# Gate projections by seven block products in a stage of their own ahead of attention, with the fill of the attention heads dealt anew

## The chip, the cores and the metric

The kernel runs on one core of one Trainium2 chip. The metric is the time of one execution on the device in microseconds, the median of the runs shown. Engines are named as in the profile: PE (TensorE, its weight loads apart as PEld), DVE (VectorE), ACT (ScalarE), POOL (GpSimd) and SP, whose queue issues the DMAs.

## The reference, cut to what matters

One decoder layer, sequence 1024, width 1024, in float32: half a SwiGLU feed-forward, two attention mixers side by side with gates, half a SwiGLU feed-forward, and a gated per-layer input.

```
x = x + 0.5 * swiglu(rms_norm(x, ffn1_norm), ffn1_w_gate, ffn1_w_up, ffn1_w_down)
h = rms_norm(x, mix_norm)
fq, fk, fv, f_logit, sq, sk, sv, g_fox, g_sb = split_columns(h @ w_in)
y_fox = forgetting_attention(rms_norm(fq), rms_norm(fk), fv, log_sigmoid(f_logit + forget_bias))
y_sb  = stick_breaking_attention(sq, sk, sv)
merged = sigmoid(g_fox) * (y_fox @ w_branch_fox) + sigmoid(g_sb) * (y_sb @ w_branch_sb)
x = x + merged @ w_out
x = x + 0.5 * swiglu(rms_norm(x, ffn2_norm), ffn2_w_gate, ffn2_w_up, ffn2_w_down)
out = x + sigmoid(rms_norm(x, ple_norm) @ w_ple_gate) * (p @ w_ple_proj)
```

Each mixer has 8 heads of 64. The gates `g_fox` and `g_sb` are 2 x 1024 of the 5128 columns of `w_in`. Forgetting attention is causal softmax with a bias from cumulated forget logs; stick-breaking attention weighs key s for query t by `beta[t,s] * prod_{s<j<t} (1 - beta[t,j])`, a running product from the diagonal to the left.

## The kernel before, in words

**Precision.** Every float32 operand is split into a high part in fp32r and a low remainder; a product is three: high x high, high x low, low x high. `split` (L103) does that: ACT copies the high part, DVE (or POOL, for weights, `wlow`, L139) subtracts it.

**Feed-forwards.** `ffn` computes up and gate as pairs of 128-column tiles for two halves of the tokens. All pairs but the first use seven block products instead of eight (Winograd's scheme): 12 products of 128x512 for each block, 84 for a pair where plain sums take 96. The operand sums on the token side (`combo_a`, `t`, `l`, `u`, `s`, `d`, `e`) are made once, at the stage's start; the sums on the weight side (`sums`, `last_sum`) for each pair. The first pair is done in plain sums (`plain`, L428) while the token sums are built. The products are at L473. `second_entry` opens the second feed-forward in the last products of the output projection; the down projection (`make_down`, L368) has the scheme too.

**The mix stage.** At the end of the first `ffn`, `mix_start` normalises x, transposes it to `hT`, and computes the first v group (`u1`) and the first q/k pair (`u2`). What else `w_in` gives is cut into units for PE, each with its weights' load and split: `v_units` (8 units of 24 products, 256 columns), `fox_qk_units` (the same), `fox_stack_units` (two units of 4 transposes), `sb_stack_units` (two units of 24 products of 128x512, for a stick-breaking head's q and k) and `g_units` (a gate tile of 128 columns: two half-tile units of 24 products of 128x512, L708). A gate unit ends with a copy (L831) or a sigmoid (L833) and a store to the scratch `gates`; `gated` loads fox gates again and applies the sigmoid there.

**Attention.** Sixteen heads in order, 0 to 7 forgetting, 8 to 15 stick-breaking; each has four steps c = 0 to 3, of two query blocks of 128. A step is `scores` for its own rows (L944, L945) and then `apply` for the step before it. In `apply`, for each pair of key blocks from the diagonal down to 0: PE transposes the weights (`transposes`, L996), ACT makes the high part (L998), DVE the low part (L999), PE multiplies with v (`values`, L1018). In stick-breaking heads `scores` has two sigmoids for each segment (ACT, L952 and L953), running products by scans on DVE (L920) and multiplications on POOL (L967, L971). The scans of the even row block come at once; those of the odd one, `right` and `left`, are put into `later` and stand in DVE's order between the low parts of `apply`. At each step's end the head's result is copied out (L1037, L1038).

Each head h has a list `fill[h]` of such units, of what later heads need, and of gates. `take` hands out 1/22 of the list's cost after each row block's scores, after each pair's transposes and before the last values, so the list lasts to the head's end:

```
        turn_and_scan(c)
        for kpair in range(c - 1, -1, -1):
            turn_and_scan(kpair)
            values(kpair + 1)
        for part in later:
            part()
        fill()
        values(0)
```

**What orders the work.** PE's order is the program's, held by `order`; so are the order of scans and low parts of stick-breaking heads on DVE, and of their high parts on ACT. The rest of attention is placed by the framework's scheduler; inside `ffn` and its entry and end the order is written out by hand. SBUF tiles come from tags with a fixed number of buffers (`BUFS`; PT has 3), and a new tile waits until the readers of the old one are done.

Of the kernel before, what the change touches and what calls it, by code (L numbers as in the profile page):

```python
# [18 lines left out]
P = 128  # L19
# [7 lines left out]
NH = 8  # L27
# [4 lines left out]
        "Q": 2, "KH": 2, "KL": 2, "Y": 2, "PT": 3}  # L32
# [4 lines left out]
def tile_hybrid_decoder_layer(  # L37
# [223 lines left out]
    def halves(N):  # L261
        return [(n["hi"], n["lo"]) for n in N]
# [117 lines left out]
    def ffn(N, wg, wu, wd, next_gain, resid, hid, tags, entry, tail):  # L380

        wsrc = [kp(w[0]) for w in (wg, wu)]
        wdown = wd[0].rearrange("(j k p) n -> k p j n", k=2, p=P)
        LA = 4
        nm_ = 2 * NF  # L390
# [4 lines left out]
        seqn += [(n, 1), (n - 1, 4), (n, 2), (n, 6), (n, 5), (n, 7), (n - 1, 3), (n, 3), (n, 4)]  # L395
# [9 lines left out]
        def load(n):  # L405
            f0 = n // 2 * 256
            W[n] = {"r": [slot(t, [P, 4, 256]) for t in tags["raw"].get(n, (("WH", "WH"), ("KH", "KL"))[n % 2])]}
            for kh in range(2):
                nc.sync.dma_start(W[n]["r"][kh][:], wsrc[n % 2][:, 4 * kh:4 * kh + 4, f0:f0 + 256])
# [23 lines left out]
        def silu(f_, half):  # L433
            if 0 not in E:
                E[0] = [slot(t, [P, 2, 512]) for t in ("GF", "RN")]
            nc.scalar.activation(E[0][f_][:, half, :], bank_of.pop("plain")[:], AF.Silu)
# [11 lines left out]
        def prep(n, m):  # L448
# [9 lines left out]
            if m == 3 and n + 2 < nm_:  # L458
                load(n + 2)
# [19 lines left out]

        def right(t, b, k):  # L480
            if isinstance(t, list):
                return t[2 * b + k // 2][:, k % 2, :]
            return t[:, b, k, :]

        def evict(n, m, ps):
# [8 lines left out]
            elif m == 7:  # L494
                nc.scalar.copy(e2[:, 1, :], ps[:])
                nc.vector.tensor_add(e2[:, 1, :], e2[:, 1, :], bank_of[n, "d"][:])
# [27 lines left out]
        C = {"w": {}, "t1": {}}  # L524

        def combo_a(q):

            h = N[1]["h"][q]
            cs = slice(q * P, (q + 1) * P)
            if q == 0:  # L530
                B[1], B[2] = N[0]["B"]
                B[3] = [slot("T", [P, 2, 512], F32R) for _ in range(4)]
                B["12"] = slot("X", [P, 2, 4, 512], F32R)
            w = C["w"][q] = slot(tags["w"][q], [P, 2, 4, P])
            v12, v22 = (turn(h, b, bank(cyc("t", ("pf", "av", "pf", "sc", "pt", "av", "pt", "sc")))) for b in range(2))
            nc.scalar.copy(w[:, 0], v12)
            nc.scalar.copy(w[:, 1], v22)
            split(B["12"][:, 0, :, cs], B["12"][:, 1, :, cs], w[:, 0], nc.scalar, nc.vector)
            for i in range(2):
                split(B[3][i][:, :, cs], B[3][2 + i][:, :, cs], w[:, 1, 2 * i:2 * i + 2], nc.scalar, nc.vector)  # L540

        def combo_t(q):

            cs = slice(q * P, (q + 1) * P)
            if q == 0:
                B[5] = slot("H", [P, 2, 4, 512], F32R)
            if q % 2 == 0:
                C["t1"][q // 2] = slot(("RN", "GF")[q // 2], [P, 2, 4, P])
            w, t1 = C["w"][q], C["t1"][q // 2][:, q % 2]
            nc.vector.tensor_sub(t1, w[:, 0], f(B[1][:, 0, :, cs]))  # L550
            nc.vector.tensor_sub(t1, t1, f(B[1][:, 1, :, cs]))
            nc.scalar.copy(B[5][:, 0, :, cs], t1)

        def combo_l(q):

            cs = slice(q * P, (q + 1) * P)
            nc.vector.tensor_sub(B[5][:, 1, :, cs], C["t1"][q // 2][:, q % 2], f(B[5][:, 0, :, cs]))

        def combo_u(q):

            w, t1 = C["w"][q], C["t1"][q // 2][:, q % 2]
            nc.vector.tensor_sub(w[:, 0], w[:, 1], w[:, 0])
            nc.vector.tensor_sub(w[:, 1], w[:, 1], t1)

        def combo_s(q, m):

            cs = slice(q * P, (q + 1) * P)
            if q == 0:
                B[m] = slot("H" if m == 6 else "X", [P, 2, 4, 512], F32R)
            split(B[m][:, 0, :, cs], B[m][:, 1, :, cs], C["w"][q][:, 7 - m], nc.scalar, nc.vector)  # L570

        def combo_d(q):

            cs = slice(q * P, (q + 1) * P)
            w = C["w"][q]
            nc.vector.tensor_sub(w[:, 0], f(B[2][:, 0, :, cs]), w[:, 1])
            nc.vector.tensor_add(w[:, 0], w[:, 0], f(B[2][:, 1, :, cs]))

        def combo_e(q):
            cs = slice(q * P, (q + 1) * P)  # L580
            if q == 0:
                B[4] = slot("X", [P, 2, 4, 512], F32R)
            split(B[4][:, 0, :, cs], B[4][:, 1, :, cs], C["w"][q][:, 0], nc.scalar, nc.vector)

        down = make_down(wdown, hid, [(0, 4), (4, 7), (7, 11)], 0.5, ("Y", "PT"))
        nxt = []

        def last_norms(i, t):
            if i == 4:
                norm_stat(nxt[0], t, ("PT", "PT", "KH", "KL")[t])  # L590
            elif i == 5:
                norm_mul(nxt[0], t)
            elif i == 6:
                if t == 3:
                    norm_post(nxt[0], 2, ps1)
                norm_stat(nxt[1], t, ("GF", "RN", "KH", "KL")[t])
                if t:
                    if t < 3:
                        norm_mul(nxt[1], t - 1)
                    norm_post(nxt[0], (None, 0, 1, 3)[t], ps1)  # L600
                for call in tail.get((i, t), ()):
                    call(nxt)

        manual[0] = True
        with tc.manual_schedule():
            entry(dict(a=combo_a, t=combo_t, l=combo_l, u=combo_u, s=combo_s, load=load, prep=prep, sums=sums, last_sum=last_sum, plain=plain, silu=silu, product=product, evict=evict))
            for s, (n, m) in enumerate(seqn):
                evict(n, m, product(n, m))
                if s == 0:
                    sums(2, nc.vector)  # L610
                    for q in range(4):
                        combo_s(q, 7)
                elif s == 2:
                    last_sum(1, nc.vector)
                    last_sum(2, nc.vector)
                if 1 < s < 6:
                    combo_d(s - 2)
                if 2 < s < 7:
                    combo_e(s - 3)
                if s + LA < len(seqn):  # L620
                    prep(*seqn[s + LA])
# [22 lines left out]
            for s, (c, i) in enumerate(steps):  # L644
# [18 lines left out]
                if final:  # L663
                    if i == 3:
                        nxt.append(norm_begin(X[0], next_gain))
                        nxt.append(norm_begin(X[1], next_gain, nxt[0]))
                    for call in tail.get(i, ()):
                        call(X)
                for t in range(4):
                    matmuls(t)  # L670
                    evict_down(t)
                    if final:
                        last_norms(i, t)
            norm_mul(nxt[1], 2)
            norm_mul(nxt[1], 3)
            tail["end"](X, nxt)
        manual[0] = False
        return X, nxt
# [302 lines left out]
    def apply(step, fill, later=()):  # L981
# [48 lines left out]
        for part in later:  # L1030
            part()
# [517 lines left out]
```

## Time and profile before

| | before |
|---|---|
| median of 3 runs | 2273.08 us (2272.70 to 2273.09) |
| profiled execution | 2274.11 us, its span 2272.4 us |
| granted TensorE clock | 1.0 |
| heads 0 to 7 (forgetting) | 755.7 to 1049.7 us |
| heads 8 to 14 (stick-breaking) | 1049.7 to 1341.7 us |
| head 15 to the end of attention | 1341.7 to 1393.3 us |

The span runs from the first instruction of the profiled execution to the last; the execution's time is somewhat longer. In rows of the timeline the first number is the start in us, the second the length; in brackets stands how long the engine had been idle and what ended that. In rows of groups the numbers after the bar are busy us in all and mean ns of one, and then idle time before them. In rows of windows stand the stretch, its length, and the busy time of PE, PEld, DVE, ACT and POOL, then the clock, the DMA engines' share and GB/s.

### The profile page before, as it was taken

The numbers are of one execution on the slowest core, as the hardware profiler recorded it, in microseconds if no ns is written. First come the engines' busy times: TensorE is split into PE (matmuls) and PEld (weight loads), VectorE is DVE, ScalarE is ACT, GpSimd is POOL, SyncE is SP. The second block draws the span as 40 slices with busy tenths as digits, with TensorE's granted clock in tenths as the row PEclk, the third lists the DMA queues.
The fourth block names the chain that finished last, engine by engine and source line by source line (L and its number), as shares of the span: only waits on it lengthen the run. The fifth ranks groups of instructions, "written<-read, shape, count | busy, mean of one in ns | idle before, by whom it ended". The sixth has DMA issues, their size and how long they took to land. (4 is left out here: it accounts for less than half of the span.)

```text
span 2272.4 us, 30639 instructions
## 1 busy us (share of the span) xinstructions
PE 2248.2 (99%) x11462; PEld 1911.9 (84%) x11462; DVE 1462.3 (64%) x2199; ACT 977.4 (43%) x1741; POOL 828.8 (36%) x762
## 2 busy tenths in 40 slices
PE   8999999999999999999999999999999999999999
PEld 6888888888899999988988888888888888888888
DVE  8845555688863466666667676889655555778753
ACT  6333333333353555555555564246333333434431
POOL 2344444300033456554645644410544444200121
PEclk9999999999999999999999999999999999999999
DMA  4232323484333322132224245822423232756132
GB/s 139 99 120 85 124 84 125 152 302 171 103 122 121 103 80 75 48 89 70 52 56 116 61 144 176 299 109 65 139 84 125 84 125 80 263 194 218 60 103 84
DMA packets 187655, 275.49 MB, mean 121 GB/s; under 512 B 27113, under 2 KB 109417, under 8 KB 187506
## 3 DMA queue, kind: packets, MB, share of 16 engines
q1 hardware_dynamic: 187504, 273.53, 35.9%
q8 instruction: 90, 1.47, 0.3%
q14 instruction: 59, 0.48, 0.1%
q10 hardware_dynamic: 2, 0.00, 0.0%
HBM read 189.83 MB, written 75.27 MB: 117 GB/s over the span
## 5 line engine op out<-in xcount | busy, mean ns | idle before, releaser
L368 PE MATMUL ps<-H,H 128*128 128x512 f32 x2184 | 497.7, 389 | 1.2 <-DVE X L376 1.2
L368 PEld LDWEIGHTS ps<-H,H 128*128 128x128 f32 x2184 | 409.4, 188 | 86.7 <-issue 2.0
L473 PE MATMUL ps<-H,WL 128*128 128x512 f32 x1008 | 239.3, 389 | 0.8 <-ACT WL L105 0.8
L473 PEld LDWEIGHTS ps<-H,WL 128*128 128x128 f32 x1008 | 189.1, 188 | 40.4 <-ACT WL L105 1.2
L708 PE MATMUL ps<-H,WH 128*128 128x512 f32 x768 | 210.3, 401 | 1.1 <-DVE PT L831 1.1
L708 PEld LDWEIGHTS ps<-H,WH 128*128 128x128 f32 x768 | 136.4, 188 | 24.1 <-DVE PT L831 1.5
L139 POOL TENSOR_TENSOR WL<-RAW,WH 128x512 fp32r<-128x512 f32 (+1 forms) x108 | 127.4, 1200 | 77.5 <-ACT WH L129 71.9
L139 POOL TENSOR_TENSOR WL<-Y,WH 128x512 fp32r<-128x512 f32 (+1 forms) x10 | 14.4, 1466 | 382.6 <-ACT WH L129 382.6
L999 DVE TENSOR_TENSOR PT<-ps,PT 128x512 fp32r<-128x512 f32 (+1 forms) x160 | 101.1, 633 | 76.1 <-ACT PT L998 75.1
L473 PE MATMUL ps<-H,Q 128*128 128x512 f32 x600 | 143.1, 389 | 0.0
L376 DVE SCALAR_TENSOR_TENSOR X<-ps,X 128x512 f32<-128x512 f32 x168 | 109.0, 685 | 50.9 <-PE ps L368 50.9
L700 PE MATMUL ps<-WH,H 128*128 128x256 f32 (+1 forms) x896 | 132.0, 287 | 1.9 <-DVE X L106 1.0
L473 PEld LDWEIGHTS ps<-H,Q 128*128 128x128 f32 x600 | 112.6, 188 | 23.4
L998 ACT CAST PT<-ps 128x512 fp32r<-128x512 f32 (+1 forms) x160 | 87.3, 548 | 95.8 <-PE ps L996 92.3
L473 PE MATMUL ps<-X,WL 128*128 128x512 f32 x504 | 121.1, 389 | 0.0
L700 PEld LDWEIGHTS ps<-WH,H 128*128 128x128 f32 x896 | 116.9, 190 | 3.7 <-DVE X L106 1.4
L1018 PE MATMUL ps<-PT,X 128*128 128x256 f32 (+1 forms) x640 | 106.2, 283 | 6.1 <-DVE PT L999 6.0
L473 PEld LDWEIGHTS ps<-X,WL 128*128 128x128 f32 x504 | 94.6, 188 | 19.6
L1018 PEld LDWEIGHTS ps<-PT,X 128*128 128x128 f32 x640 | 94.5, 190 | 19.1 <-DVE PT L999 9.7
L708 PE MATMUL ps<-H,WL 128*128 128x512 f32 x384 | 108.3, 398 | 0.0
L957 POOL TENSOR_TENSOR T<-T,l 128x128 f32<-128x128 f32 (+3 forms) x64 | 73.3, 1150 | 88.5 <-DVE l L956 86.1
L269 POOL TENSOR_TENSOR PT<-GF,RN 128x512 f32<-128x512 f32 x20 | 33.1, 1655 | 186.0 <-DVE GF L516 101.8
(400 smaller groups left out, 4735.3 us busy)
## 6 DMA issues: line engine op xcount, KB each, us to landing
hidden<-PT SPq DMA_DIRECT2D x40, 512.0 KB, 3.1
WH<-in_ffn_w_gate_dram SPq DMA_DIRECT2D x38, 512.0 KB, 5.3
Q<-hidden SPq DMA_DIRECT2D x24, 512.0 KB, 6.1
hidden<-RN SPq DMA_DIRECT2D x22, 512.0 KB, 2.7
RAW<-in_w_in_dram SPq DMA_DIRECT2D x22, 512.0 KB, 4.3
KH<-in_ffn_w_up_dram SPq DMA_DIRECT2D x20, 512.0 KB, 6.2
KL<-in_ffn_w_up_dram SPq DMA_DIRECT2D x20, 512.0 KB, 6.8
T<-in_ffn_w_down_dram SPq DMA_DIRECT2D x20, 512.0 KB, 4.3
```

What stands on the lines that cost most here:

```text
L139: ins = eng_lo.tensor_sub(lo[part], raw[part], f(hi[part]))
L269: eng.tensor_add(s12[:, 0, :], g1[:, 1, :], g2[:, 1, :])
L368: pe(nc.tensor.matmul(groups[g][t][:], act[:, a, k, t * P:(t + 1) * P], wt[:, b, k, :], start=(fresh and n == 0), stop=(i in (6, 1, 4) and ...
L376: nc.vector.scalar_tensor_tensor(xs, groups[g][t][:], scale, xs, ALU.mult, ALU.add)
L473: pe(nc.tensor.matmul(ps[:], hl[:, a, k, :], rhs(m, b, k), start=(first and i == 0), stop=(final and i == 11), skip_group_check=True))
L700: pe(nc.tensor.matmul(ps[:, :n], hT[t // 4][a][:, k, (t % 4) * P:(t % 4 + 1) * P], w[k // 4][b][:, k % 4, :n], start=(i == 0), stop=(i == ...
L708: pe(nc.tensor.matmul(ps[:], w[a][:, k, :], hT[half][b][:, k, :], start=(i == 0), stop=(i == 23)))
L957: nc.gpsimd.tensor_mul(T[:, :n], T[:, :n], l[:].broadcast_to([P, n]))
L998: high = nc.scalar.copy(pt[:, 0, :width], ps[:, :width])
L999: low = nc.vector.tensor_sub(pt[:, 1, :width], ps[:, :width], f(pt[:, 0, :width]))
L1018: pe(nc.tensor.matmul(o, lh, r, start=(kpair == c and i == 0), stop=(kpair == 0 and i == 3)))
```

## The change

- The gate tiles 0 to 11 leave attention. After the first `ffn` comes a stage of six pairs of gate tiles (`NG = 6`), written like the start of the second feed-forward, from which the shared parts are taken out (`make_up`, `up_order`, `up_begin`, `up_step`, `up_first`, `products`). Pair 0 is done in plain sums, pairs 1 to 5 by seven block products. Its results get the sigmoid at once and are stored.
- `hT` is now read from the operands of that stage (`B[1]`, `B[2]`, `B["12"]`, `B[3]`), whose homes are other tags than in the feed-forwards. All of `u1` runs at the stage's end, all of `u2` at the start of attention.
- Gate tiles 12 to 15 stay fill units. The fill lists are dealt anew, with stacks further behind their q and k units.
- `values` of a key pair come one more pair behind its transposes, and PT has five buffers.
- The sigmoid of fox gates moves from `gated` to `g_units`.

```diff
-        "Q": 2, "KH": 2, "KL": 2, "Y": 2, "PT": 3}
+        "Q": 2, "KH": 2, "KL": 2, "Y": 2, "PT": 5}
...
             g = slot("PT", [P, 512])
-            if m < KD:
-                nc.vector.tensor_copy(g[:], ps[:])
-            else:
-                order("act", nc.scalar.activation(g[:], ps[:], AF.Sigmoid))
+            order("act", nc.scalar.activation(g[:], ps[:], AF.Sigmoid))
...
             turn_and_scan(kpair)
-            values(kpair + 1)
+            if kpair + 2 <= c:
+                values(kpair + 2)
         for part in later:
             part()
+        if c:
+            values(1)
         fill()
         values(0)
...
+    NG = 6
...
+        tags_g = {"raw": UP_TAGS["raw"], "sum": UP_TAGS["sum"], "w": UP_TAGS["w"], "hl": hl, "t1": "X",
+                  "B": {"12": "H", 3: "H", 5: ("Y", "Y", "PT", "PT"), 6: ("T",) * 4, 7: "X", 4: "X"}}
+        F = make_up(N, lambda n: kp(win)[:, :, GFOX + n * 256:GFOX + n * 256 + 256], NG, tags_g, AF.Sigmoid, gate_out, load_qk)
...
+        def end():
+            up_first(N, F)
+            seqn = up_order(NG)
+            L = len(seqn)
+            for s, (n, m) in enumerate(seqn):
+                evict(n, m, F.product(n, m))
+                F.begin(s)
+                if s + 4 < L:
+                    F.prep(*seqn[s + 4])
+                if s == L - 16:
+                    raws["v"] = [wraw_load(pieces[kh], 4, 256 + NH, "PT") for kh in range(2)]
+                elif s == L - 5:
+                    mx["v"]["w"] = [wsplit(raws["v"][kh], 4, 256 + NH, ("T", "WL")) for kh in range(2)]
+                elif s == L - 2:
+                    mx["qk"]["w"] = [wsplit(raws["qk"][kh], 4, 256, tags[kh]) for kh in range(2)]
...
+            for _, g in mx["u1"]:
+                run(g)
...
-        run_all(g0[:1] + f0[:1] + p0[1:3] + g0[1:] + f0[1:] + p0[3:] + g1[:1] + p1 + g1[1:])
-        fill = []
-        fill.append(mix(fst(1), fox_qk_units(fox_pairs[1], qk[1])))
...
-        u, g6 = sst(8), g_units(6)
-        fill.append(u + g6)
-        u, g7, g8 = sst(9), g_units(7), g_units(8)
-        fill.append(u + g7 + g8[:1])
-        u, uv = sst(10), v_units(SV + 256, 0, vs1)
-        fill.append(u + g8[1:] + uv[:4])
-        u, g9 = sst(11), g_units(9)
-        fill.append(uv[4:] + u + g9[:1])
-        u, g10 = sst(12), g_units(10)
-        fill.append(u + g9[1:] + g10)
-        u, g11, g12 = sst(13), g_units(11), g_units(12)
-        fill.append(u + g11 + g12[:1])
-        u, g13 = sst(14), g_units(13)
-        fill.append(u + g12[1:] + g13)
-        u, g14, g15 = sst(15), g_units(14), g_units(15)
-        fill.append([u[0], g14[0], g15[0], u[1], g14[1]])
-        fill.append(g15[1:] + fox_branch[:7])
+        run_all(f0[:1] + p0[1:7] + f0[1:] + p0[7:] + p1)
...
+        fill = [mix(f[0], qk1[:7]),
+                qk1[7:] + vx[:1] + f[1][:1] + vx[1:4] + f[1][1:],
+                mix(f[2], vx[4:] + uq2[:3]),
+                uq2[3:] + g12[:1] + f[3][:1] + g12[1:] + f[3][1:],
+                mix(f[4], uq3[:6]),
+                uq3[6:] + vy[:1] + f[5][:1] + vy[1:4] + f[5][1:],
+                mix(f[6], vy[4:] + g13[:1]),
+                g13[1:] + s8,
+                s9 + vz[:2],
+                vz[2:5] + s10,
+                vz[5:] + s11,
+                s12 + g14[:1],
+                g14[1:] + s13,
+                s14 + g15[:1],
+                g15[1:] + s15,
+                fox_branch[:7]]
...
         nc.sync.dma_start(dst, gd[gate * KD + m, :, half * 512:half * 512 + 512])
-        order("act", nc.scalar.activation(dst, dst, AF.Sigmoid))
         nc.vector.tensor_mul(dst, dst, ps[:])
...
-    nc = _bacc.Bacc("TRN2", target_bir_lowering=False, num_devices=1, dynamic_dma_scratch_size=8192)
+    nc = _bacc.Bacc("TRN2", target_bir_lowering=False, num_devices=1, dynamic_dma_scratch_size=4096)
```

In the entries of the old list that are left out here stood gate tiles 2 to 5; tiles 0 and 1 were computed ahead of the list.

More of the change, by code (lines that the diff above doesn't have):

```diff
@@ L522, in hidden_sums @@
             del E[n], E[n - 1]
[L524 to L540, printed above, removed]
```

501 lines of the change are left out of this document (287 added, 214 removed).

## The prediction, made before the changed kernel was run

> **What bounds the kernel now.** I read the page first, then the chain of waits in order of time, then windows cut by stage and by step of attention, then the timelines of one step.
>
> ```profile
> span 2272.4 us, 30639 instructions
> ...
> PE 2248.2 (99%) x11462; PEld 1911.9 (84%) x11462; DVE 1462.3 (64%) x2199; ACT 977.4 (43%) x1741; POOL 828.8 (36%) x762
> ...
> PE 46%; DVE 2%; ACT 1%; issue 0%; DVEq 0%; ACTq 0%
> ```
>
> TensorE is busy 99% of the span, and the 46% is only as far back as the chain could be followed; DVE's 2% is the first hint of a second bound. The next views say how fast PE runs undisturbed, and how full the others are in attention.
>
> ```profile
> 1566.89 394.40 PE ps L473 x1740
> 755.72:1049.73 294.01, 289.80 (x2074) 271.34 (x2073) 180.11 (x563) 159.91 (x346) 166.75 (x169) 1.00 0.25 70
> 1049.73:1341.74 292.01, 288.42 (x1639) 249.26 (x1637) 195.59 (x279) 160.13 (x337) 164.70 (x181) 1.00 0.29 80
> 1341.74:1393.33 51.59, 49.22 (x272) 41.89 (x271) 40.20 (x54) 34.96 (x70) 28.25 (x34) 1.00 0.56 185
> PE ps L1018 <- DVE PT L999: 6.0, 10, 1.7
> ```
>
> The first row is from the chain in order of time: 1740 products of 128x512 in 394.40 us, 0.2267 us each. The next three are windows (length, then PE, weight loads, DVE, ACT, POOL busy, granted clock): the eight forgetting heads 0 to 7, the stick-breaking heads 8 to 14, and head 15 to the end of attention. PE is covered by fill, but DVE is at 61%, 67% and 78%. The last row, from the waits of PE in attention, is the only large one: value products (L1018) waiting ten times, 6.0 us in all, for the low part that DVE makes (L999). So PE's number of products bounds the kernel, with little lost; and what attention can do with less fill is set by DVE.
>
> **The change, part by part.**
>
> *Fewer products.* Before, 12 gate tiles cost 12 x 48 = 576 products of 128x512. After, the first two tiles are four plain sums of 24, and five pairs take seven blocks of 12: 96 + 420 = 516. At 0.2267 us the 60 fewer are **-13.6 us**. The stage is 516 x 0.2267 = 117 us of PE ahead of attention, and 130.6 us of fill leaves it.
>
> *The stage itself.* It runs the code that opens the second FFN, whose first 120 us and whose entry the trace shows:
>
> ```profile
> 1535.28 1.09 PE L228 MATMUL ps<-identf,PT 128*128 128x128 f32 x8 [0.99 <-DVE H L106]
> 1536.77 1.09 PE L228 MATMUL ps<-identf,PT 128*128 128x128 f32 x8 [0.40 <-ACT Q L536]
> 1566.90:1687.00 120.10, 120.10 (x531) 99.47 (x531) 81.89 (x104) 47.59 (x85) 47.23 (x33) 1.00 0.30 103
> 603.00:640.00 37.00, 37.00 (x165) 30.64 (x164) 28.65 (x31) 19.10 (x24) 10.84 (x12) 1.00 0.38 129
> RAW<-in_w_in_dram SPq DMA_DIRECT2D x22, 512.0 KB, 4.3
> ```
>
> After the entry PE stood busy for all 120.10 us, with DVE at 68% beside it: the operand sums (113 more DVE instructions and 16 fewer copies in the whole kernel) are hidden there, and would cost their time only if PE had waits. The entry idled 0.99 + 0.40 us; the old end of the first FFN, 603 to 640, idled nothing. So **+1.4 us**, bounds +1 and +5 (the homes of the operands differ, and the v and q/k weights are now split at its end). The loads and stores of x, gates and weights go through SP's queue as before, two tiles, some 14 products or 38 us, ahead, and land in 4.3 us: nothing.
>
> *Less fill in stick-breaking heads: the term that decides.* A head's fill is dealt in 22 equal portions: 7 in step c0, 4 in c1, 5 in c2, 6 in c3. Heads 8, 11, 12, 13 and 14 go from five half-tile units to three: 2 x 24 x 0.2267 = 10.9 us less, each portion 1.24 to 0.74 us. Heads 9 and 10 lose one such unit and one unit of 24 products of 256 columns, counted at half that price: 8.2 us; head 15 loses 5.4 us. Here are head 13's four steps (windows), then rows of its c3 from the timelines of DVE, ACT, PE and POOL, one scan of head 12, and a group of heads 8 to 14:
>
> ```profile
> 1258.55:1271.56 13.01, 13.01 (x76) 11.21 (x75) 5.51 (x10) 5.06 (x12) 3.43 (x6) 1.00 0.31 93
> 1271.56:1278.40 6.84, 6.84 (x36) 5.68 (x35) 3.89 (x8) 4.67 (x9) 4.08 (x5) 1.00 0.00 0
> 1278.40:1287.62 9.22, 9.22 (x52) 7.97 (x51) 8.39 (x11) 5.72 (x13) 7.77 (x9) 1.00 0.43 116
> 1287.62:1299.51 11.89, 11.89 (x65) 10.03 (x64) 9.47 (x11) 7.73 (x15) 8.43 (x8) 1.00 0.13 44
> ...
> 1293.24 0.56 DVE L999 TENSOR_TENSOR PT<-ps,PT 128x384 fp32r<-128x384 f32 x1 [0.74 <-ACT PT L998]
> 1293.72 1.12 DVE L920 TENSOR_TENSOR_SCAN RN<-GF,mask_sb 128x128 f32<-128x128 f32 x1
> 1294.87 1.01 DVE L920 TENSOR_TENSOR_SCAN RN<-GF,RN 128x383 f32<-128x383 f32 x1
> ...
> 1296.38 2.03 DVE L920 TENSOR_TENSOR_SCAN RN<-GF,RN 128x512 f32<-128x512 f32 x1
> 1298.33 0.66 DVE L999 TENSOR_TENSOR PT<-ps,PT 128x512 fp32r<-128x512 f32 x1
> ...
> 1288.27 0.55 ACT L952 ACTIVATE GF<-ps 128x448 f32<-128x448 f32 x1
> ...
> 1292.21 0.63 ACT L833 ACTIVATE PT<-ps 128x512 f32<-128x512 f32 x1
> 1292.68 0.53 ACT L998 CAST PT<-ps 128x384 fp32r<-128x384 f32 x1
> ...
> 1298.85 0.82 PE L1018 MATMUL ps<-PT,X 128*128 128x256 f32 x4
> ...
> 1293.55 1.00 POOL L971 TENSOR_TENSOR T<-T,RN 128x384 f32<-128x384 f32 x1
> 1248.50 0.43 DVE L920 TENSOR_TENSOR_SCAN RN<-GF,mask_sb 128x128 f32<-128x128 f32 x1 [1.10 <-ACT GF L952]
> ...
> L785 DVE TENSOR_TENSOR KL<-ps,KH 64x512 fp32r<-64x512 f32 x14 | 9.7, 695 | 0.3
> ```
>
> With the smaller portions PE's own work is 13.01 - 3.5 = 9.5, 6.84 - 2.0 = 4.9, 9.22 - 2.5 = 6.7 and 11.89 - 3.0 = 8.9 us. DVE has 5.5, 3.9, 8.4 and 9.5 us: in c0 and c1 it has room, in c2 and c3 together it has 17.9 us against 15.6. Every step ends with values(0), which needs the last low part; that low part stands behind all scans of the step in DVE's order, and the change keeps that order. So what DVE lacks in c2 and c3 cannot be paid back in c0.
>
> How much is it? In c3 the chain runs thus: eight sigmoids from 0.65 us after the step's start to 4.6 (ACT with hardly a break, so less fill does not hurry them), the high part 0.5, then DVE without a pause from the first low part (1293.24) to the last (1298.99), 5.75 us, then the last values, 0.45. That is 11.3 us against PE's 8.9: 2.4 us. It falls to 1.0 if the scans run at their shortest: 0.43 us for the 1.12, and for 512 columns at the pace of the 383 in 1.01, 1.35 for the 2.03. PE already started its last values at 1298.85, before that low part was done: there is no slack to spend. In c2, 8.4 against 6.7 bounds the loss by 0 and 1.7; I take 0.6, as part of the last scan runs over into c3. In c1 I take 0.1 (bounds 0 and 0.5). The stacks make it worse at the upper end: one half of the next head's (two subtractions of about 0.7 us) now falls behind c2's last scan in DVE's order as built, where it stood in c0 and c1 (+1.4). So 3.1 us a head, bounds 0.8 and 4.5: five heads 15.5; heads 9 and 10, with three quarters of the cut, 1.5 each (0 and 2.5); head 15, where DVE's 40.20 of 51.59 us is full already, 2.5 (1.7 and 4.5). The longest wait that stands there now, 1.7 us, may go. **+19 us**, bounds +4 and +32.
>
> The value products now come a key pair later (five PT buffers instead of three). That takes away waits for a low part in the middle of a step; the last one has only a portion and four products more ahead of it, which is in the 8.9 us.
>
> On the scans: one of 128 columns took 0.43 us with POOL idle (1248.50), and 1.12 when a POOL multiplication had begun 0.17 us earlier; it ended 0.3 us after that one did. I keep the long ones, since the same multiplications follow the same scans after the change. [...]
>
> *Less fill in forgetting heads.* Their fill goes from about 23 to between 14 and 25 us; head 1 loses most, three units of 24 products of 256 columns, 8.2 us (a window, and a group):
>
> ```profile
> 789.58:827.09 37.51, 37.03 (x303) 36.46 (x302) 23.51 (x72) 21.16 (x46) 22.17 (x23) 1.00 0.21 57
> L883 ACT ACT_TABLE_LOAD x1 | 1.3, 1283 | 0.0
> ```
>
> 37.5 - 8.2 = 29.3 us of PE against 23.5 of DVE: room is left, and there are no scans between low parts. I take 0.5 us in five heads and 1 in head 1, **+3.5 us** (bounds -1, if the later values remove waits, and +6). Four sigmoids of gate tiles 12 and 13 now fall between exponentials of these heads: eight table loads more there, 1.28 us each on ACT (one more, at the gate stage, is hidden). ACT has 16 us free even in that head; I take **+1 us**, bounds 0 and 8 x 1.28 = 10.3.
>
> *Sum.* -13.6 + 1.4 + 19 + 3.5 + 1 = **+11 us** on the profiled execution, 2274.1 (span 2272.4 and 1.7 around it), that is 2285; the median of the three runs is 2273.1, 1 us lower: **2284 us**.
>
> **Rivals.** *PE still decides.* If ACT's and DVE's chains start as much earlier as PE does, and the scans run at their short durations, the losses are the lower bounds: -13.6 + 1.4 + 4 - 1 + 0 = -9, **2264 us**, faster. For it speaks that the later values and five buffers loosen every wait but the last of a step; against it, 17.9 us of DVE in 15.6 of PE. It decides when c2 and c3 together end less than 1 us late in each head.
>
> *The attention heads fall apart.* The stack halves lie in DVE's way in every c2 and the table loads, 10.3 us on ACT, hold up the high parts that values wait for: -13.6 + 3 + 28 + 6 + 8 = +31, **2304 us**. For it: ACT's 23.2 us would fill 77% of head 13; against it: the loads fall in only three heads. [...]
>
> *It comes out even.* Half of the 19 us in the stick-breaking heads, 1.4 at the entry and 2.5 in the forgetting heads make 13.4 against the 13.6: **2273 us**; the fill would then be worth to attention just what the blocks save.
>
> **How the numbers follow.** A measurement here tells about 0.2%, 4.5 us, from no change. Forecast 0.50, PE decides 0.30, even 0.12, falls apart 0.08. Slower than 2277.6: 0.50 + 0.08 = 0.58; within: 0.12; faster: 0.30. The forecast's own range is 2275 to 2298; as 0.30 lies on the other side, the range reaches from 2262 to 2304.
>
> **What would show it.** Right: the new stage runs PE full at 0.2267 us a product for 117 us, with under 3 us of idle time at its entry; heads 11 to 14 last 33 to 34 us instead of 41; PE's waits for the low part grow from 6 to over 20 us, nearly all at the ends of c2 and c3; DVE is at 80 to 88% of these heads. Wrong: these heads last 31 us or less (PE decides); or PE's idle time lies in the gate stage, or in heads 3, 6 and 7 behind a table load.

## The result, and the profile after

| | before | after |
|---|---|---|
| median | 2273.06 us (2272.70 to 2273.09, 4 runs) | 2324.7 us (2322.22 to 2327.65, 4 runs) |
| profiled execution, its span | 2274.11, 2272.4 us | 2324.22, 2322.3 us |

The ratio is 1.0228, 95% interval 1.0215 to 1.024: the kernel became slower by 51.6 us. The sign was forecast, the size was not: 11 us, and the upper end of the range was 2304.

First the page's head and busy lines of the changed kernel, then windows of its gate stage, heads 0 to 7, heads 8 to 14, and head 15 with the rest of attention.

```profile
span 2322.3 us, 30570 instructions
...
PE 2255.0 (97%) x11402; PEld 1909.7 (82%) x11402; DVE 1526.4 (66%) x2296; ACT 1018.1 (44%) x1819; POOL 811.4 (35%) x747
```

```profile
640.00:757.00 117.00, 115.99 (x543) 96.22 (x542) 86.04 (x134) 61.32 (x117) 15.64 (x17) 1.00 0.34 114
851.30:1144.30 293.00, 267.25 (x1927) 249.84 (x1926) 173.00 (x550) 168.57 (x355) 159.08 (x162) 0.98 0.22 60
1144.30:1392.60 248.30, 223.95 (x1330) 192.12 (x1329) 198.14 (x277) 150.14 (x324) 150.27 (x170) 0.99 0.25 69
1392.60:1442.70 50.10, 46.74 (x247) 39.30 (x247) 40.61 (x56) 24.46 (x52) 29.57 (x31) 0.95 0.52 176
```

TensorE has 60 instructions fewer, as planned, and is full in the gate stage. In attention it is not: 25.8 us of heads 0 to 7 and 24.4 of heads 8 to 14 are empty, and the granted clock, 1.00 throughout before, is 0.98, 0.99 and 0.95. Set beside the times of before, with a gate tile at 48 products of 0.2267 us, the difference splits thus:

| stretch | length before | length after | TensorE's work moved | lost |
|---|---|---|---|---|
| start to the first scores | 755.7 | 851.3 | 516 products in, tiles 0 and 1 out: +95.2 | 0.4 |
| heads 0 to 7 | 294.0 | 293.5 | three tiles out: -32.6 | 32.1 |
| heads 8 to 15 | 343.6 | 297.9 | seven tiles out: -76.2 | 30.5 |
| the rest | 879.1 | 879.6 | none | 0.5 |

The moved work is -13.6 in all, the loss 63.5, together the 49.9 us by which the spans differ. So heads 0 to 7 gave nothing back at all for three gate tiles less. The 32.1 us lost there lie in all eight heads, 1.8 to 7.2 us in each, with the most in heads 4 and 6. TensorE stands still 21.5 us longer than before, and its remaining products take 10.6 us longer, in part because of the half clock shown below. (The windows above end 0.4 us before head 8 begins; the table goes by the first scores.)

Line numbers are higher in the changed kernel: L1092, L1094, L1095 and L1114 are transposes, high parts, low parts and values; L799 and L807 the products of fill units; L889, L106 and L929 the evictions of stacks, v and gates; L1016 the scans.

These are the waits of TensorE in heads 0 to 7 of the changed kernel (us in all, times, the longest), then the largest of heads 8 to 15:

```profile
PE ps L799 <- DVE KL L889: 7.1, 3, 2.8
PE ps L1092 <- DVE PT L1095: 5.3, 6, 1.4
PE ps L799 <- DVE X L106: 4.5, 4, 1.8
PE ps L807 <- ACT PT L929: 1.6, 1, 1.6
PE ps L1114 <- DVE PT L1095: 1.6, 2, 1.2
PE ps L1114 <- ACT PT L1094: 1.5, 1, 1.5
PE ps L1092 <- POOL T L1053: 1.2, 2, 0.8
```

```profile
PE ps L1114 <- DVE PT L1095: 23.2, 24, 1.8
```

The second is the wait that the prediction named: value products for the last low part, 6.0 us before, 23.2 now. The first list has no leader: fill units that wait for the eviction of a stack (KL), of v (X) or of a gate (PT, L929), transposes and values that wait for high and low parts. And this is how such a wait looks in the timeline of TensorE, at the start of head 4:

```profile
999.83 0.66 PE L901 MATMUL ps<-identf,RN 128*128 128x128 f32 x4 [0.94 <-ACT PT L929]
1003.26 0.98 PE L799 MATMUL ps<-WH,H 128*128 128x256 f32 x3 [2.78 <-DVE KL L889]
...
1004.46 1.70 PE L799 MATMUL ps<-WH,H 128*128 128x256 f32 x7
...
1010.11 1.08 PE L799 MATMUL ps<-WH,H 128*128 128x256 f32 x7
```

After 0.94 and 2.78 us of standing still, seven products take 1.70 us; the same seven take 1.08 later. The granted clock is 0.5 from 1002.1 to 1008.9 us, and in four other places of attention: 23.9 us in all at half speed.

### The profile page after: what moved, and what is told of

Read it like the earlier page. It is cut to its first block, busy times and chain, and to the rows that moved or that the text cites. A ratio compares the mean times of both kernels' runs of the same rounds, so it can differ in the third digit from the quotient of the medians.

```text
span 2322.3 us, 30570 instructions
## 1 busy us (share of the span) xinstructions
PE 2255.0 (97%) x11402; PEld 1909.7 (82%) x11402; DVE 1526.4 (66%) x2296; ACT 1018.1 (44%) x1819; POOL 811.4 (35%) x747
## 4 chain that ended last, share of the span: by engine, by line
PE 85%; DVE 8%; ACT 4%; issue 2%; POOL 1%; DMA 0%; SPq 0%; ACTq 0%; DVEq 0%; POOLq 0%
PE ps L556 38%; PE ps L454 21%; PE ps L799 7%; PE ps L1556 4%; DVE RN L1016 3%; PE ps L1361 3%; PE ps L1114 2%; PE ps L807 2%; PE ps L506 2%; PE ps L1092 2%; DVE PT L1095 1%; PE ps L959 1%; PE ps L228 1%; PE ps L1040 1%; PE ps L1041 1%
## 5 line engine op out<-in xcount | busy, mean ns | idle before, releaser
L556 PE MATMUL ps<-H,WL 128*128 128x512 f32 x1116 | 265.0, 389 | 0.8 <-ACT WL L105 0.8
L556 PEld LDWEIGHTS ps<-H,WL 128*128 128x128 f32 x1116 | 209.4, 188 | 44.7 <-ACT WL L105 1.2
L1095 DVE TENSOR_TENSOR PT<-ps,PT 128x512 fp32r<-128x512 f32 (+1 forms) x160 | 99.9, 629 | 61.9 <-ACT PT L1094 60.9
L556 PEld LDWEIGHTS ps<-H,Q 128*128 128x128 f32 x612 | 114.9, 188 | 23.9
L799 PE MATMUL ps<-WH,H 128*128 128x256 f32 x768 | 121.7, 296 | 12.2 <-DVE KL L889 7.1
L1114 PE MATMUL ps<-PT,X 128*128 128x256 f32 (+1 forms) x640 | 106.8, 288 | 27.3 <-DVE PT L1095 24.7
L556 PE MATMUL ps<-X,WL 128*128 128x512 f32 x552 | 132.6, 389 | 0.0
L1114 PEld LDWEIGHTS ps<-PT,X 128*128 128x128 f32 x640 | 91.0, 190 | 42.2 <-DVE PT L1095 34.1
L139 POOL TENSOR_TENSOR WL<-RAW,WH 128x512 fp32r<-128x512 f32 (+1 forms) x84 | 99.0, 1201 | 74.6 <-ACT WH L129 42.1
L556 PEld LDWEIGHTS ps<-X,WL 128*128 128x128 f32 x552 | 103.6, 188 | 21.5
L799 PEld LDWEIGHTS ps<-WH,H 128*128 128x128 f32 x768 | 105.5, 197 | 15.3 <-issue 7.7
L1094 ACT CAST PT<-ps 128x512 fp32r<-128x512 f32 (+1 forms) x160 | 87.0, 551 | 65.6 <-PE ps L1092 62.9
L807 PE MATMUL ps<-H,WH 128*128 128x512 f32 x384 | 111.6, 404 | 1.6 <-ACT PT L929 1.6
L556 PE MATMUL ps<-H,PT 128*128 128x512 f32 x456 | 108.8, 389 | 0.0
L1016 DVE TENSOR_TENSOR_SCAN RN<-GF,RN 128x127 f32<-128x127 f32 (+2 forms) x96 | 102.8, 1071 | 2.6
L1092 PE MATMUL ps<-identf,T 128*128 128x128 f32 x576 | 92.6, 278 | 10.6 <-DVE PT L1095 7.7
```

What stands on the lines that cost most here:

```text
L139: ins = eng_lo.tensor_sub(lo[part], raw[part], f(hi[part]))
L556: pe(nc.tensor.matmul(ps[:], hl[:, a, k, :], rhs(m, b, k), start=(first and i == 0), stop=(final and i == 11), skip_group_check=True))
L799: pe(nc.tensor.matmul(ps[:, :n], hT[t // 4](a, k)[:, (t % 4) * P:(t % 4 + 1) * P], w[k // 4][b][:, k % 4, :n], start=(i == 0), stop=(i == ...
L807: pe(nc.tensor.matmul(ps[:], w[a][:, k, :], hT[half](b, k), start=(i == 0), stop=(i == 23)))
L1016: order("dve", nc.vector.tensor_tensor_scan(*args))
L1092: pe(nc.tensor.transpose(ps[:, col:col + P], step["pr"][j][:, kb * P:(kb + 1) * P], identf[:]))
```

## The experiments

Each edit is to the changed kernel (2324.7) unless it says otherwise; ranges are over the runs of each, and the kernel before ran at 2273.1 to 2273.2 beside all of them.

**Stack units apart.**

```diff
-                qk1[7:] + vx[:1] + f[1][:1] + vx[1:4] + f[1][1:],
+                qk1[7:] + f[1][:1] + vx[:2] + f[1][1:] + vx[2:4],
...
-                uq2[3:] + g12[:1] + f[3][:1] + g12[1:] + f[3][1:],
+                uq2[3:] + f[3][:1] + g12[:1] + f[3][1:] + g12[1:],
...
-                uq3[6:] + vy[:1] + f[5][:1] + vy[1:4] + f[5][1:],
+                uq3[6:] + f[5][:1] + vy[:2] + f[5][1:] + vy[2:4],
```

> The changed kernel, with the two stack units of heads 2, 4 and 6 drawn apart in the lists of heads 1, 3 and 5, so that two units of 24 products lie between them and none of them stands at the list's end. Theory 1 (two short stack units back to back on two banks stop the fill, and TensorE's clock halves after the gap): step c0 of heads 2, 4 and 6 gets its 3.7, 6.8 and 3.5 us back, the half-clock stretches at 920, 1002 and 1077 us are gone, and the time falls from 2324.7 by 10 to 16, to about 2312. Rival (it is the sigmoids of gate tiles 12 and 13 that hold the banks, or the later values): under 4 us less, and the gaps in c0 of heads 4 and 6 remain.

2324.47 us (2323.82 to 2325.78): nothing. Step c0 of heads 2, 4 and 6 did get 3.7, 1.9 and 3.6 us back, but head 1 grew by 4.2 and head 3 by 2.1. In all, heads 0 to 7 took 2.5 us less, and heads 9 and 12, into which half-clock stretches fell (mean clock of the execution 0.995), took 1.4 and 1.3 us more. Theory 1 fell as a cause of its own: where the units stand decided mostly where TensorE waits, and little of how much.

**Tiles 12 and 13 without their sigmoid.**

```diff
-            order("act", nc.scalar.activation(g[:], ps[:], AF.Sigmoid))
+            if m < 14:
+                order("act", nc.scalar.copy(g[:], ps[:]))
+            else:
+                order("act", nc.scalar.activation(g[:], ps[:], AF.Sigmoid))
```

> The changed kernel, with gate tiles 12 and 13 stored by a plain copy: their sigmoid is left out, and with it the eight table loads among the exponentials of heads 3, 4, 6 and 7. Theory 2 (the loads hold up the evictions behind them): the waits of TensorE for these tiles' evictions go, 6 to 12 us less, about 2316. Rival (the loads are hidden beside ACT's free time, and the gaps come from the stack units): within 3 us of 2324.7, and the half-clock stretches stay where they are.

2315.58 us (2312.39 to 2318.71), 9.1 less. The table loads are not hidden, as theory 2 had it. They are these two groups:

```profile
L929 ACT ACT_TABLE_LOAD x4 | 5.1, 1283 | 5.1 <-PE ps L807 5.1
L1051 ACT ACT_TABLE_LOAD x4 | 5.1, 1283 | 0.1
```

Eight loads of 1.28 us are 10.3; within the spread of these runs, some 3 us, nearly all of it came through to the end. This is one of them in the timelines of ACT and TensorE of the changed kernel:

```profile
985.33 1.28 ACT L929 ACT_TABLE_LOAD   x1 [0.95 <-PE ps L807]
986.62 0.60 ACT L929 ACTIVATE PT<-ps 128x512 f32<-128x512 f32 x1
987.24 1.28 ACT L1051 ACT_TABLE_LOAD   x1
...
987.27 0.50 PE L807 MATMUL ps<-H,WH 128*128 128x512 f32 x1 [1.59 <-ACT PT L929]
```

All four loads at L929 begin after a wait for the gate's products (5.1 us in all, 0.95 here), and the next gate products wait 1.59 us for the eviction behind this one.

**Values one key pair behind, as before.**

```diff
-            if kpair + 2 <= c:
-                values(kpair + 2)
+            values(kpair + 1)
...
-        if c:
-            values(1)
         fill()
         values(0)
```

> The changed kernel, with the values again one key pair behind the transposes as in the kernel before; PT keeps five buffers. If the later values are what hurts (more transposes ahead of them on two banks, so that transposes wait for low parts): 5 us or more faster, under 2320. If they help, as the prediction assumed: waits for low parts come back in the middle of steps and the time is 2325 to 2340.

2321.44 us (2320.51 to 2324.07): between the two expectations, and overlapping with the changed kernel. The later values neither help nor hurt by more than some 3 us.

**The fill of before put back.** The lists of before stand in place of the new ones, and `g_units` copies tiles below 8.

> The changed kernel with its gate stage, but with the fill lists of the kernel before: gate tiles 2 to 15 are computed in attention once more, those below 8 stored by a copy. It has 20 half-tile units (109 us) more for TensorE than the changed kernel, gate tiles 0 and 1 not being repeated. If the loss is the lack of fill and its order: attention lasts as before, 638 us from the first scores to the last value products, and the time is 2273 - 20 (u1 and the four half-tiles of tiles 0 and 1 are elsewhere or gone, about 21.8 us) + 117 + 1.4 = about 2370. If the later values, the five buffers or the stage itself cost the time: attention stays some 60 us longer than that, about 2430.

2369.71 us (2369.49 to 2370.03), and attention lasts 637.1 us as against 637.6 before, with a clock of 1.0 throughout. So the stage costs what its products cost, the later values and the five buffers cost nothing with this fill, and the whole loss is due to the fill: its amount, its order, and whether its gates end with a copy or a sigmoid.

**Stick-breaking heads: DVE's scans.** First without the left scans, then with POOL's multiplications cut to 128 columns.

```diff
-                    scan(R[:, 0:cut][:, ::-1], G[:, 1:cut + 1][:, ::-1], G[:, 1:cut + 1][:, ::-1], R[:, cut:cut + 1], ALU.mult, ALU.bypass)
-                    nc.gpsimd.tensor_mul(T[:, :cut], T[:, :cut], R[:, :cut])
+                    nc.gpsimd.tensor_mul(T[:, :cut], T[:, :cut], G[:, :cut])
```

> The changed kernel without the left scans of stick-breaking heads (the running product over the left part of a row is left out; POOL multiplies by the sigmoids themselves, so its work and the order stay). It takes 0.7 to 2.0 us of DVE out of each of the row blocks 3 to 7, about 1.7 in c2 and 3 in c3. Theory 3 (DVE's order sets the end of c2 and c3 in these heads): c2 falls from 7.6-9.1 to about 7, c3 from 11.8 to 9-10, 3 to 4.5 us a head, some 24 to 32 us in all, about 2297. Rival (the wait is for ACT's sigmoids, or the small portions of fill): under 10 us.

2307.77 us (2305.84 to 2309.98), 16.9 less: c3 of heads 11 to 13 falls from 11.9 to 10.0 us, as expected; c2 does not fall everywhere, so less came back than forecast. Of the 44.7 us of scans that are gone, 24.0 lay in c2, and the eight c2 steps together became only 1.5 us shorter (68.3 to 66.8); the 21.3 us out of c3 made the c3 steps 12.3 us shorter.

```diff
-                    nc.gpsimd.tensor_mul(T[:, cut:n - 1], T[:, cut:n - 1], R[:, cut:n - 1])
+                    e = min(cut + P, n - 1)
+                    nc.gpsimd.tensor_mul(T[:, cut:e], T[:, cut:e], R[:, cut:e])
...
-                    nc.gpsimd.tensor_mul(T[:, :cut], T[:, :cut], R[:, :cut])
+                    nc.gpsimd.tensor_mul(T[:, :P], T[:, :P], R[:, :P])
```

> The changed kernel with POOL's multiplications of stick-breaking heads cut to 128 columns of each part (the weights of the other columns are left unmultiplied); the scans, the order and the waits stay. If a scan is held up while POOL multiplies, as the prediction read from 0.43 and 1.12 us for the same scan: the scans of c3 get shorter by 1.4 us together, those of c2 by some 0.5, and the time falls by about 9 to 15, to 2312. If the two do not disturb each other: the scans keep their lengths, and only waits for POOL's result go, under 3 us.

2307.18 us (2305.45 to 2308.42), 17.5 less, without any DVE instruction changed. Groups of scans in the changed kernel, and the same groups with the short multiplications (busy us, mean ns of one):

```profile
L1016 DVE TENSOR_TENSOR_SCAN RN<-GF,mask_sb 128x128 f32<-128x128 f32 x56 | 35.7, 637 | 2.5 <-ACT GF L1048 1.6 <-POOL T L1063 0.6
L1016 DVE TENSOR_TENSOR_SCAN RN<-GF,RN 128x384 f32<-128x384 f32 x16 | 19.7, 1232 | 0.3
L1016 DVE TENSOR_TENSOR_SCAN RN<-GF,RN 128x512 f32<-128x512 f32 x8 | 15.9, 1988 | 0.0
```

```profile
L1016 DVE TENSOR_TENSOR_SCAN RN<-GF,mask_sb 128x128 f32<-128x128 f32 x56 | 29.6, 528 | 4.7 <-ACT GF L1048 4.0 <-POOL T L1068 0.4
L1016 DVE TENSOR_TENSOR_SCAN RN<-GF,RN 128x384 f32<-128x384 f32 x16 | 16.4, 1027 | 0.3
L1016 DVE TENSOR_TENSOR_SCAN RN<-GF,RN 128x512 f32<-128x512 f32 x8 | 10.2, 1274 | 0.0
```

All scans together go from 141.9 us to 119.6, by 9.8 in c2 and 12.9 in c3. That scans take longer beside long POOL multiplications, which the prediction read from two rows, is now shown: 1988 ns against 1274 for 128x512, 637 against 528 for 128x128. That DVE's scans hold up the end of c3 is shown by both runs, for c3 became shorter in each. For c2 it is not: what sets its end was not taken apart.

**Fill dealt late in heads 8 to 15.**

```diff
+        share, at = (0.55, 0.55, 1.4, 1.5), [0]
...
-                state[0] += total / 22
+                state[0] += total / 22 * (share[at[0]] if h > 7 else 1.0)
```

> The changed kernel, with the fill of heads 8 to 15 dealt unevenly: portions of 0.55 of the mean in c0 and c1, 1.4 in c2, 1.5 in c3. Theory 3 (c0 and c1 have TensorE's time to spare, c2 and c3 wait for DVE): c0 falls by about 2.3 and c1 by 1 us, c2 and c3 grow by far less than the 1.5 and 2.2 us added, a head takes 31 to 32.5 us instead of 34 to 36, and the time falls by 10 to 20, to about 2310. Rival (the heads are bound by all of their work together, or the stack halves pushed into c2 and c3 eat the gain): under 5 us.

2315.43 us (2314.33 to 2316.82), 9.3 less. c0 fell by 0.9 to 2.8 us and c1 by 1, but c3 rose to 12.5 to 15.1, so the heads take 33 to 35.6 us, not 31 to 32.5. The direction is theory 3's, at half the size.

**Forgetting heads: one suspect at a time.** A third bank for the fill:

```diff
     def fill_bank():
-        return bank("pf")
+        third[1] += 1
+        return bank("sc" if third[0] and third[1] % 3 == 0 else "pf")
```

> The changed kernel, with every third fill unit of heads 0 to 7 in a bank of the scores (three banks) instead of the fill's two. If the fill stops because two banks are not free again in time behind ACT's exponentials: the waits of TensorE for v, stack and gate evictions, about 15 us in the trace of the changed kernel, mostly go, with two half-clock stretches: 10 to 18 us less, about 2310. Rival (whatever gives way, the heads wait for the same chain of scores, exponentials and low parts): within 5 us, the waits return at the scores or the transposes.

2325.6 us (2324.0 to 2326.74): nothing. Next, POOL's power and multiplication of the q/k norm (2.9 and 1.9 us each) left out:

```diff
-                nc.gpsimd.tensor_tensor(ss, ss, mhalf[:], ALU.pow)
-                nv = N[:].rearrange("p a h s d -> p (a h s) d")
-                nc.gpsimd.tensor_mul(nv, nv, ss.unsqueeze(2).broadcast_to([P, 16, HD]))
+                nv = N[:, 0, 0, 0, 0:1]
+                nc.gpsimd.tensor_mul(nv, nv, ss[:, 0:1])
```

> The changed kernel with POOL's normalisation of q and k in heads 0 to 7 cut to one element (the scaling by the norm is left out): a power of 2.9 us and a multiplication of 1.9 us, twice for each pair of heads, leave POOL's queue, where they stand ahead of the masks that the first maxima need. Theory POOL (in forgetting heads with little fill the chain scores, mask, maximum, exponential, multiplication, transposes is late wherever POOL is held up): heads 1, 3 and 5 each get 2 to 4 us back, 6 to 12 in all with the half-clock stretches, about 2315. Rival (the chain is late by ACT's and DVE's queues alone): within 3 us of 2324.5.

2320.81 us (2319.63 to 2323.19), 3.9 less, short of the 6 to 12 expected: heads 2 to 5 get 1.0 to 2.0 back each, head 1 nothing. Up to 1.6 us in one head can be a half-clock stretch that fell elsewhere in that execution (last section), and head 2 shows the same 1.6 in the run without the sigmoid, so the shares of single heads say little. Then ACT's order:

```diff
+                def soft(T=T, m=m, l=l, n=n, k=nm_):
+                    order("act", nc.scalar.activation(T[:, :n], T[:, :n], AF.Exp, bias=m[:, k - 1:k], scale=-1.0, accum_out=l[:]))
...
+                if i % 2 and later is not None:
+                    later.append(soft)
+                else:
+                    soft()
...
+            order("act", high)
```

> The changed kernel, with the exponential of the second row block of each step in heads 0 to 7 put behind the first high copy of the step before it, and this order held on ACT. Theory ACT (high parts wait in ACT's queue behind exponentials whose maxima are not ready): waits for ACT's and DVE's parts of PT shrink, 5 to 12 us less, about 2316. Rival (the exponentials are then late by as much as the high parts come earlier, or POOL is what they wait for): within 4 us.

2322.35 us (2320.27 to 2324.57), 2.4 less, within the spread of the runs. Head 3 loses 3.7, the other seven gain 0.3 to 2.7 each.

**All four together** (stacks apart, no sigmoid of 12 and 13, no norm on POOL, ACT's order):

> The changed kernel with four earlier edits together: stack units apart, tiles 12 and 13 stored by a copy (their sigmoid left out), POOL's normalisation of q and k left out, high parts between the exponentials. If the waits are causes of their own that add up: the forgetting heads lose under 10 us instead of 32, and the time falls by 20 to 28, to about 2300. If they stand in for each other: the sigmoids' 9 us and little more, about 2313.

2303.65 us (2302.05 to 2304.88), 21.1 less: together they take 21 of the 32 us, with TensorE's products unchanged. The medians of the four alone add up to less (0.2 + 9.1 + 3.9 + 2.4 = 15.6), but each is uncertain by some 2 to 3 us, and heads 0 to 7 alone, in the profiled executions, became 2.5, 10.1, 6.3 and 3.9 us shorter, 22.8 in all, against 21.4 together. So it is not shown that the four need one another. Heads 1 to 7 take 239.5 us instead of 260.5, and the half-clock time falls from 23.9 to 6.8 us, the mean clock of the execution 0.994 and 0.998. Against TensorE's own work about 11 of the 32 us remain.

**The old fill in heads 0 to 7 alone.** The lists of before there: 144 products, 32.6 us of TensorE, more than in the changed kernel. The sigmoid of tiles 12 and 13, and with it the eight table loads, is left out here too.

> The changed kernel with the lists of the kernel before in heads 0 to 7: four more gate tiles are computed there again (tiles 2, 3, and 4, beside 12 and 13 that stand there already; all stored by a copy, the sigmoid of 12 and 13 left out), some 32 us more for TensorE. If fill in these heads is only cover for other engines: heads 0 to 7 take 294 us as in both kernels, and the time stays at 2324.5 within 4. If the losses have to do with the order or the tables alone, the heads get 20 to 32 us longer: 2345 to 2357.

2326.53 us (2325.43 to 2327.46): 32.6 us more work and no table loads cost 2 together. Against the run without the sigmoid (2315.58), where the loads are gone as well, the work cost 11. The window of heads 0 to 7, but for their last 1.6 us:

```profile
851.40:1144.30 292.90, 288.42 (x2065) 269.51 (x2064) 178.94 (x561) 160.62 (x348) 166.66 (x168) 1.00 0.26 71
```

The heads take 294.5 us, where the changed kernel took 293.5 and the run without the sigmoid 283.3, and TensorE is now busy nearly throughout at a clock of 1.00. So about two thirds of the three gate tiles are free here: TensorE does them while it would otherwise wait. The order of the fill changed with its amount, and the two were not taken apart.

**A faster version: before, with its fill dealt late.** The edit is that of the late fill above, in the kernel before, with (0.85, 0.85, 1.15, 1.2):

> The kernel before, its fill in heads 8 to 15 dealt with weights 0.85, 0.85, 1.15 and 1.2 for c0 to c3. By theory 3 the 6 us that TensorE waits there for low parts at the ends of c2 and c3 shrink, since more fill lies ahead of the last values, and c0 and c1 have room: 2 to 6 us less than 2273.1. If the waits are set by DVE's whole order and only move: 2273, within 1.5.

2264.99 us (2264.64 to 2265.21, 5 runs), ratio 0.9964 (0.995 to 0.9978): 8.1 less than before, the fastest kernel here. First the window of heads 8 to 14, then the wait for low parts in heads 8 to 15:

```profile
1048.60:1333.60 285.00, 285.00 (x1637) 248.61 (x1637) 202.32 (x279) 161.66 (x337) 169.88 (x181) 1.00 0.29 82
```

```profile
PE ps L1018 <- DVE PT L999: 1.3, 2, 0.9
```

TensorE is busy for all 285.00 us, where the 292.01 of before held 288.42; the wait falls from 6.0 to 1.3. With 0.7, 0.7, 1.3 and 1.4:

> As the one before, with weights 0.7, 0.7, 1.3 and 1.4. If the stack halves are not pushed behind the scans of c2: 3 to 8 us less than 2273.1; if they are, DVE's chain in c2 and c3 gets 0.7 us longer for each subtraction and the time is 2273 or above.

2266.18 us (2266.11 to 2268.09), ratio 0.9972 (0.9962 to 0.9983). Heads 8 to 14 take as long as with the milder weights, but head 15 takes 53.1 us instead of 50.3, in an execution 1.9 us above the median, with a half-clock stretch in that head (mean clock 0.999). Beyond the point where c2 and c3 are covered there is nothing to win.

**A smaller gate stage with fill dealt late** (tiles 0 to 5, old lists in heads 0 to 7, four tiles fewer in heads 8 to 15):

> A gate stage of three pairs only (tiles 0 to 5; NG = 3), the lists of the kernel before in heads 0 to 7 with tiles 6 to 10 stored by a copy and their sigmoid applied where they are loaded, tiles 11 to 15 in heads 8 to 15 with some 21.5 us of fill in each of heads 8 to 13, dealt 0.75, 0.75, 1.25, 1.25. The fill that is gone came out of c0 and c1 alone. From the 2265 of the kernel before with late fill: 24 products fewer are -5.4, the stage's entry +1.4, and heads 8 to 15 lose 0 to 6 if c2 and c3 are covered as before: 2262, between 2258 and 2268. If every us of fill taken away costs 0.4, as on average in the changed kernel: 40 us less fill are +16, about 2277.

2285.98 us (2284.73 to 2286.48), ratio 1.0055 (1.0041 to 1.0068): missed by 24 us, and nearer to the price of 0.4 for each us of fill. From the faster version it is 21 us away: -5.4 for the products, +6.9 up to the first scores (one wait in the stage is 2.8 us, and half clock follows; the mean clock of the execution is 0.998), 0.6 in heads 0 to 7, and 18.9 in heads 8 to 15, which return 24.6 us for 43.5 of fill. In heads 8, 11, 12 and 13 c2 takes 10.7 us, where the kernel before had 9.2 with portions of the same size: taking fill out of c0 and c1 alone did not leave c2 as it was. Which of the works pushed into c2 makes the difference was not taken apart. Where the new order of fill leaves most of these 21 us, in heads 8 to 15, a stage does not pay.

## Why the prediction was wrong

*Fewer products, the stage, its entry: right.* -13.6 us of products; 0.4 lost up to the first scores, where 1.4 was forecast. (The first scores came at 755.7 us before, and at 754.4 and 755.1 in the two faster versions, whose code is the same up to there, so the loss is 0.4 to 1.7.) The old fill put back shows the same from the other side.

*Stick-breaking heads: the right mechanism, mis-sized.* +19 was forecast, 30.5 came. The wait is the one named (23.2 us for low parts), DVE is at 80% of heads 8 to 14, and heads 11 to 14 take 35.2, 34.0, 33.9 and 36.2 us, the forecast 33 to 34. Heads 9 and 10 lost 1.8 and 1.9 (forecast 1.5), head 15 3.9 (2.5), but the other five 3.1 to 6.0 (3.1). Three things made the size wrong. In c2 the loss reached 2.3 us in heads 8 and 11 against 0.6 taken and a bound of 1.7; since taking 24.0 us of scans out of c2 hardly shortened it, DVE's sum was not the right measure there, and the cause stays open. In c3 heads 8, 11, 12 and 13 lost 2.1 to 3.5 us against 2.4. And after such waits the granted clock fell to 0.5: three of the seven half-clock windows lie in these heads, up to an estimated 1.5 us each (below).

*Forgetting heads: the step that failed.* +3.5 and +1 were forecast, bounds -1 to 16.3; 32.1 came. The step compared busy times in head 1, 29.3 us of TensorE against 23.5 of DVE, and took the difference for room; that head then took 32.2 us, and heads 4 and 6 lost 7.2 and 6.4. These heads are a chain through all engines (scores, mask on POOL, maximum on DVE, exponential on ACT, multiplication on POOL, transposes, high part, low part, values), and fill is what TensorE does during the chain. Two runs bear this out: with TensorE's work unchanged, less work and another order on the other engines gave 21.1 us back, and 32.6 us more fill cost 11 where the loads are left out on both sides. The table loads, taken at 1 us with their upper bound at 10.3, cost 9.1. "ACT has 16 us free" was true of its sum and no help, since each load, 1.28 us, stood ahead of an eviction or an exponential, and TensorE waited 1.59 us for one such eviction. Stack units, POOL's norm and ACT's order make up the rest of the 21.1 us; how it divides among them is not shown, since alone each gained 0.2 to 3.9 us, with a spread of some 2 to 3. What holds the last 11 us was not taken apart.

*The rivals.* "The attention heads fall apart" was nearest, 2304, with the right suspects (table loads, stacks) and too small a bound for the forgetting heads, 6 us and 8. "PE still decides" is refuted by every window of attention; its condition, c2 and c3 less than 1 us late, failed in each of these heads.

*Scans beside POOL.* The prediction put the loss of a c3 at 2.4 us, and at 1.0 with the scans at their shortest, so their longer times beside POOL at 1.4 us for each c3. The short multiplications were worth 22.3 us of scans and 17.5 us of time, though a part of the 17.5 can be POOL's results being ready earlier. The price was too low in the prediction: it counted c3 alone, whose scans fell by 12.9 us, and left out c2, whose scans fell by 9.8. How a multiplication makes a scan longer is not shown.

## What to carry to other kernels

Fill is not free to take: before moving work out of a stage that it covers, ask of each step how long its chain is through all engines, not how busy each of them is. Put back into heads 0 to 7 of the changed kernel, 32.6 us of work cost 11, both sides without the table loads. And when a stage waits at the ends of its long steps, deal the same fill later before changing its amount: one line of weights was worth 8.1 us, where saving 13.6 us of products lost 51.6.

## What was not expected of the hardware

In the changed kernel the longest that TensorE stood still in attention was 2.8 us, and its granted clock fell to 0.5 five times there. In the run with the values one key pair behind, it did so after two pauses of 1.10 and 1.08 us close together:

```profile
1174.78 0.62 PE L1114 MATMUL ps<-PT,X 128*128 128x256 f32 x3 [1.10 <-DVE PT L1095]
...
1177.32 0.72 PE L1114 MATMUL ps<-PT,X 128*128 128x256 f32 x3 [1.08 <-DVE PT L1095]
...
1178.15 2.02 PE L799 MATMUL ps<-WH,H 128*128 128x256 f32 x8
...
1181.93 1.08 PE L799 MATMUL ps<-WL,H 128*128 128x256 f32 x7
```

The half clock lasts from 1177.7 to 1181.1 us here; eight products take 2.02 us, seven 1.08 when it is over. In the changed kernel the half-clock stretches of attention begin at 920.2, 1002.1, 1077.2, 1169.3 and 1391.2 and last 3.41 or 6.83 us; their starts lie 24, 22, 27 and 65 times 3.41 us apart. Cut on that grid, the window ahead of each of these five was idle for 1.80 to 2.53 us, over half of it; one more window of attention, idle for 1.81, had no half-clock stretch behind it, nor had any with 1.6 or less, but for the ones already at half clock. In the run of the rows above the window ahead was idle for 1.59. So no sharp limit is shown.

Step c0 of head 9 took 10.4 us in the changed kernel and 11.9 in this one, where the half clock falls into it. A cleaner pair is head 6 of the changed kernel and of the run without left scans, whose instructions are the same up to there: 37.6 us with a half-clock window, 36.1 without. But head 5 of these two took 35.4 in both, though the second has a half-clock window in it, at 1052.3 us. So a window costs from nothing to about 1.5 us, at most some 10 for the seven of the changed kernel, an estimate from these pairs; and since the stretches fall otherwise in each of these executions (neither 1177.7 nor 1052.3 is a whole number of 3.41 us away from 1077.2), a difference of this size in one head of one profile need not come from the edit.
